# The last gate columns and the output projection go into the ordered list of a two-layer decoder trunk, with two of eight pairs of the projection by seven products

## Chip, cores and metric

The kernel runs on one core of one Trainium2 chip. The metric is the device time of one execution in microseconds; of several runs the median is taken. The engines are called as in the profile: PE is the matmul engine (TensorE), DVE is VectorE, ACT is ScalarE, POOL is GpSimd, and SP (SyncE) issues the DMAs.

## What is computed

The trunk has two layers over 256 tokens of width 2048. Each layer projects the normalised input to 6160 columns, runs eight gated linear-attention heads (GLA) and eight stick-breaking heads on them, joins their outputs, projects them back (`w_o`), and adds a squared-ReLU MLP:

```python
h = rms_norm(x, attn_norm)
g_q, g_k, g_v, g_gate, g_lr, s_q, s_k, s_v = split(h @ w_in)
...
o_gla = rms_norm(gla_chunked(...), gla_out_norm) * silu(g_gate)   # 1024 columns
o_sb  = rms_norm(stick_breaking_attention(...), sb_out_norm)      # 1024 columns
mixed = concatenate([o_gla, o_sb], axis=-1)
x = x + mixed @ w_o                                               # 2048 x 2048
hm = rms_norm(x, mlp_norm)
x = x + square(relu(hm @ w_up)) @ w_down                          # 8192 wide
```

The change touches the gate columns `g_gate`, the product `mixed @ w_o`, and how both stand to the MLP behind them.

## The kernel before

**Products.** A float32 product is made of three matmuls: weights are split into a high part (ACT, `whi`) and the rest (DVE, `wlo`), activations likewise, and a block is high x high, high x low and low x high. A matmul has 128 rows of the activation (one of two halves of the tokens, `tt`) against 512 weight columns.

**Attention part.** `unit` (L537) makes 512 columns of a projection: four loads of 512 rows of weights (1 MB each), each split in two parts, each part 12 matmuls; after each part a counter ticks, and small work that was put on the counter with `after` (head matmuls, transposes, norms) is issued there. A unit sums into one accumulator `acc`; there are two of them, of two PSUM banks each, taken in turn, beside four single banks `ps` (L197). Late in a layer come two units of GLA values (L1036), which bring `gla_pair` and `gla_out` of the last pairs; two units of gate columns (L1050); and four units of the output projection (L1077). `gate_part` (L1054) copies a unit's two banks out on ACT (L1056), makes the silu on ACT and DVE, and `gated` multiplies an `on` tile by it, which `to_operand` turns on PE into the operand `mixed`. Each of the first three projection units is added to the residual by one DVE instruction (L1075), then transposed for the MLP (`norm_operand`) and squared; the fourth is left to the list.

**Ordered list.** The MLP is written as pieces with an engine, a length and dependencies (class `Plan`, L40). `plan.run` walks a model of time, gives each ACT or DVE piece a due time from the PE pieces that need it, and writes out the instructions of PE, DVE and ACT in the order in which the model began them: whenever an engine comes free in the model, it takes the piece with the earliest due time among those that are ready at that moment. The pieces of PE and SP keep the order in which they were added. PE's last five parts ahead of the list stand in it as five pieces of 12 matmuls (`tail`, L1111), a load has 2.9 us on SP and lands 4.6 us later, an ACT piece of one part has 1.0, of one bank 0.55, and 0.06 us passes between engines.

The list's units have 1024 columns and eight pairs of 128-row blocks, four alternating passes of `w_up` and `w_down`. A plain pair (`steps`, L1200) has two parts of 12 matmuls, 24 in all, into banks 2, 4, 3 and 8. A fast pair (1, 3 and 5) has seven products in place of eight, 21 matmuls, into all eight banks m1 to m8: three sums of weight blocks on DVE (L1098, tiles `ts`, `raw`, `t`), four parts instead of two, sums of the operand's blocks (`forms`, L401), and at the end of a unit `down_tail` or `up_tail`, where the seven sums are combined.

**Memory.** Tiles with names in `ATT` (among them `kdz`, `v4` and `on`) and in `MLP` (among them `raw2`, `whi5`, `wlo5`) lie in one stretch of SBUF by turns; `open_scope` closes one set and opens the other. The list's first load of every four goes to `raw2`, its first part of every five to `whi5` and `wlo5`. `mlp_psum` (L204) closes the accumulators and opens the banks in the order m5, m7, m1, m6, m2, m4, m3, m8. These pools are opened with `reuse_waits="tile"`: a tile of the new pool waits for the old tiles whose memory it takes. Before, the SBUF set is opened ahead of the second projection unit, `mlp_psum` behind the fourth.

Of the kernel before, what the change touches and what calls it, by code (L numbers as in the profile page):

```python
# [17 lines left out]
P = 128  # L18
# [108 lines left out]
def trunk_kernel(  # L127
# [270 lines left out]
    def fast(i):  # L398
        return i in (1, 3, 5)
# [334 lines left out]
    def norm_pair(po):  # L734

        o = tmp("on", [P, 512], bufs=4)
# [39 lines left out]
    for l in range(DEPTH):  # L776
# [234 lines left out]
        def gla_out(e, v, vc, S, sc):  # L1011
# [21 lines left out]
            ons[e] = norm_pair(po)  # L1033
# [6 lines left out]
        def gated(e, gate, c):  # L1040
            o = ons[e]
            o4 = o.rearrange("p (h t d) -> p h t d", h=2, t=NT)
            for tt in range(NT):
                nc.vector.tensor_tensor(
                    o4[:, :, tt, :], o4[:, :, tt, :],
                    gate[:, tt, c : c + 2 * P].rearrange("p (h d) -> p h d", d=P), ALU.mult,
                )
            after(1, lambda: to_operand(mixed, e, o, gain("gla", l)))

        for g in range(2):  # L1050
            ug = unit(hT, wl, 0, C_GG + g * 512, 512)
            gate = act_tile(F32, (P, NT, 512))

            def gate_part(tt, ug, gate):  # L1054
                gx = gate[:, tt, :]
                nc.scalar.activation(gx, ug[:, tt, :], AF.Copy, scale=rst[:, tt : tt + 1])  # L1056
                e = tmp("t2", [P, 512], bufs=4)
                nc.scalar.activation(e, gx, AF.Abs)
                nc.scalar.activation(e, e, AF.Exp, scale=-1.0)
                nc.scalar.activation(e, e, AF.Ln, bias=1.0)  # L1060
                nc.vector.scalar_tensor_tensor(e, gx, 0.0, e, ALU.min, ALU.subtract)
                nc.scalar.activation(e, e, AF.Exp)
                nc.vector.tensor_tensor(gx, gx, e, ALU.mult)

            gate_part(0, ug, gate)
            after(1, lambda a=ug, b=gate: gate_part(1, a, b))
            for hp in range(2):
                after(3 + hp, lambda e=2 * g + hp, t=gate, c=hp * 2 * P: gated(e, t, c))


        hm = Operand()
        ssq = new_ssq()

        def residual(n, acc):
            nc.vector.tensor_tensor(xb[n], acc, xb[n], ALU.add)  # L1075

        for n in range(4):  # L1077
            uo = unit(mixed, w_o[l], 0, n * 512, 512, (2, 3, 0, 1))
            if n == 0:

                open_scope("sbuf", mlp=1)
            if n < 3:
                residual(n, uo)
                after(1, lambda n=n: norm_operand(hm, n, "mlp", l, sums=True))
                after(2, lambda n=n: norm_squares(n, ssq))
# [3 lines left out]
        mlp_psum()  # L1089
        hT = Operand()  # L1090
# [12 lines left out]
        units = [(q, down, n2) for q in range(4) for down in range(2) for n2 in range(2)]  # L1103
# [7 lines left out]
        tail = [add("PE", 12 * MM, None) for _ in range(RING)]  # L1111
        for t in tail:
            whi.append([t])
            wlo.append([t])
        x3 = add("DVE", V2, lambda: residual(3, uo), tail)

        def norm_last():

            sq = add("ACT", 2 * A1, lambda: norm_squares(3, ssq), x3)
            return norm_end(sq, ssq)  # L1120
# [13 lines left out]
        def turned(n, h2, m, op, key, ll, deps):  # L1134

            turn, high, low, _ = operand_parts(op, n, h2, key, ll, lambda: bank(m))
            a = add("PE", 8 * TR / 2, turn, deps, free.get(m))
# [5 lines left out]
        def weights(u, j):  # L1143
            q, down, n2 = units[u]
            if down:
                r0, c0, w = q * 2048, n2 * 1024, w_down[l]
            else:
                r0, c0, w = 0, q * 2048 + n2 * 1024, w_up[l]
            r0 += 2 * j * P
            return w[r0 : r0 + 2 * P, c0 : c0 + 1024].rearrange("(k p) n -> p k n", p=P)  # L1150

        def load(x):

            box = []

            def fn():
# [4 lines left out]
                nc.sync.dma_start(box[0], weights(*divmod(x, 8)))  # L1161
# [38 lines left out]
        def steps(x, r, ld, readers):  # L1200

            u, j = divmod(x, 8)
            q, down, n2 = units[u]
            op = up[q] if down else hm

            def blk(k, tt):
                sl = slice(tt * P, (tt + 1) * P)
                return lambda: (op.t[j][:, k, 0, sl], op.t[j][:, k, 1, sl])

# [3 lines left out]
            if not fast(j):  # L1213
# [57 lines left out]
        def down_tail(u):  # L1271
            q, _, n2 = units[u]
            end = q == 3 and l + 1 == DEPTH
# [44 lines left out]
        def up_tail(u):  # L1318
# [37 lines left out]
            def turn(h):  # L1356

                q, _, n2 = units[u]
# [5 lines left out]
                for i, m in enumerate(((5, 7), (1, 6))[h]):  # L1364
# [24 lines left out]
                    def made(k, box=box, h=h, i=i, pair=pair):  # L1389
                        key = "f", h, i  # L1390
                        if key not in box:
# [103 lines left out]
```

## Time and profile before

| | before |
|---|---|
| median of 3 runs | 2189.72 us (2189.27 to 2190.19) |
| profiled execution, its own time | 2190.13 us |
| span in its profile, first to last instruction | 2188.4 us |
| PE busy | 2180.2 us |
| DVE busy | 1795.7 us |
| ACT busy | 1255.3 us |
| mean granted PE clock | 1.000 |

The profiled execution takes 1.73 us more than the span that its profile shows, and is 0.41 us above the median. A row of a timeline gives the start in the span, the duration, engine, line, operation, tiles (out<-in), and in brackets the idle time ahead of it with what ended that. A matmul's duration is longer than the distance to the next one, since they overlap.

### The profile page before, as it was taken

Reading aid. Unit: us, or ns where it says so; the run is one execution under the profiler, and the core shown is the slowest. Engines: PE = TensorE matmul, PEld = TensorE weight load, DVE = VectorE, ACT = ScalarE, POOL = GpSimd, SP = SyncE. Lnnn points to the kernel's source line nnn. Section 1 sums busy time; section 2 is a strip of 40 time slices with the busy share of each in tenths; the row PEclk is TensorE's granted clock in tenths of the full one; section 3 lists DMA queues with packets and bytes.
Section 4 is the critical chain, followed back from the end, with each engine's and each line's share of the span. In section 5 each row is a group of like instructions: output and inputs, shape, how many; then the busy total and the mean of one; then the engine's idle time right before and its main releaser. Section 6 shows DMA issues by size and latency. Waiting matters only on the chain.

```text
span 2188.4 us, 27082 instructions
## 1 busy us (share of the span) xinstructions
PE 2180.2 (100%) x10376; PEld 1808.0 (83%) x10376; DVE 1795.7 (82%) x2286; ACT 1255.3 (57%) x1623; POOL 38.0 (2%) x64
## 2 busy tenths in 40 slices
PE   9999999999999999999999999999999999999999
PEld 7988778888888888888888887788888888888887
DVE  5777566799999999999957775567999999999998
ACT  5555346566566566466645553555665655665663
POOL 0020000000000000000000200000000000000000
PEclk9999999999999999999999999999999999999999
DMA  6654445566556556656546544465656665565564
GB/s 224 198 160 154 154 150 196 177 206 211 184 199 204 186 198 205 211 187 198 173 156 193 173 155 154 135 219 185 211 174 208 198 209 192 193 211 183 201 199 149
DMA packets 152549, 408.96 MB, mean 187 GB/s; under 512 B 6650, under 2 KB 31810, under 8 KB 152420
## 3 DMA queue, kind: packets, MB, share of 16 engines
q1 hardware_dynamic: 152420, 407.24, 56.7%
q8 instruction: 81, 1.33, 0.2%
q14 instruction: 48, 0.39, 0.1%
HBM read 405.12 MB, written 2.10 MB: 186 GB/s over the span
## 4 chain that ended last, share of the span: by engine, by line
PE 98%; DVE 1%; DMA 0%; issue 0%; ACT 0%; SPq 0%; POOL 0%; ACTq 0%
PE acc L549 9%; PE acc L551 9%; PE acc L550 9%; PE acc L596 3%; PE acc L600 1%; PE ps L1017 1%; PE ps L1029 1%; PE ps L441 0%; PE ps L976 0%; PE ps L712 0%; PE ps L658 0%; PE ps L747 0%; PE ps L676 0%; DMA raw<-in_w_in_dram 0%; PE ps L993 0%
## 5 line engine op out<-in xcount | busy, mean ns | idle before, releaser
L1180 ACT ACTIVATE whi<-raw 128x1024 fp32r<-128x1024 f32 x512 | 533.1, 1058 | 314.5 <-ACT whi L1180 12.1
L1184 DVE TENSOR_TENSOR wlo<-raw,whi 128x1024 fp32r<-128x1024 f32 x512 | 620.2, 1220 | 88.9 <-ACT whi L1180 84.8
L532 DVE TENSOR_TENSOR wlo<-raw,whi 128x1024 fp32r<-128x1024 f32 (+2 forms) x274 | 317.4, 1164 | 192.8 <-ACT whi L530 192.1
L530 ACT ACTIVATE whi<-raw 128x1024 fp32r<-128x1024 f32 (+2 forms) x274 | 273.6, 1005 | 292.6 <-PE acc L551 243.8
L549 PE MATMUL acc<-whi,act 128*128 128x512 f32 (+2 forms) x960 | 368.7, 384 | 1.3 <-ACT act L451 1.3
L550 PE MATMUL acc<-wlo,act 128*128 128x512 f32 (+2 forms) x960 | 362.3, 377 | 0.0
L551 PE MATMUL acc<-whi,act 128*128 128x512 f32 (+2 forms) x960 | 362.2, 377 | 0.0
L549 PEld LDWEIGHTS acc<-whi,act 128*128 128x128 f32 x960 | 181.2, 189 | 36.3 <-issue 4.1
L551 PEld LDWEIGHTS acc<-whi,act 128*128 128x128 f32 x960 | 180.8, 188 | 34.1 <-issue 0.7
L550 PEld LDWEIGHTS acc<-wlo,act 128*128 128x128 f32 x960 | 181.2, 189 | 31.1 <-issue 0.7
L1180 ACT ACTIVATE whi<-t 128x512 fp32r<-128x512 f32 x96 | 60.5, 630 | 151.6 <-DVE t L1098 150.0
L1184 DVE TENSOR_TENSOR wlo<-ts,whi 128x1024 fp32r<-128x1024 f32 x96 | 117.4, 1223 | 1.5 <-ACT whi L1180 0.3
L1098 DVE TENSOR_TENSOR ts<-raw 128x1024 f32<-128x1024 f32 x96 | 117.1, 1220 | 1.3
L1180 ACT ACTIVATE whi<-ts 128x1024 fp32r<-128x1024 f32 x96 | 101.0, 1052 | 27.4 <-PE m__662_3602 L1265 0.7
L596 PE MATMUL acc<-act,whi 128*128 128x512 f32 x256 | 91.9, 402 | 0.0
L600 PE MATMUL acc<-act,wlo 128*128 128x256 f32 x256 | 71.8, 280 | 0.0
L1184 DVE TENSOR_TENSOR wlo<-t,whi 128x512 fp32r<-128x512 f32 x96 | 65.7, 684 | 1.1 <-ACT whi L1180 1.1
L1098 DVE TENSOR_TENSOR raw<-ts,raw 128x512 f32<-128x512 f32 x96 | 65.6, 684 | 0.0
L1098 DVE TENSOR_TENSOR t<-raw 128x512 f32<-128x512 f32 x96 | 65.6, 684 | 0.0
L1349 ACT ACTIVATE act<-act,st 128x512 f32<-128x512 f32 x64 | 44.3, 716 | 26.5 <-DVE act L1098 26.5
L596 PEld LDWEIGHTS acc<-act,whi 128*128 128x128 f32 x256 | 48.1, 188 | 11.1
L600 PEld LDWEIGHTS acc<-act,wlo 128*128 128x128 f32 x256 | 48.4, 189 | 0.1
(2401 smaller groups left out, 4581.2 us busy)
## 6 DMA issues: line engine op xcount, KB each, us to landing
raw<-in_w_up_dram SPq DMA_DIRECT2D x128, 1024.0 KB, 5.1
raw<-in_w_down_dram SPq DMA_DIRECT2D x128, 1024.0 KB, 5.2
raw<-in_w_in_dram SPq DMA_DIRECT2D x84, 1024.0 KB, 5.2
raw<-in_w_o_dram SPq DMA_DIRECT2D x32, 1024.0 KB, 5.1
raw<-in_w_in_dram SPq DMA_DIRECT2D x14, 512.0 KB, 6.6
raw<-in_w_in_dram SPq DMA_DIRECT2D x8, 544.0 KB, 3.8
out_dram<-xb SPq DMA_DIRECT2D x8, 256.0 KB, 3.2
xb<-in_x_dram SPq DMA_DIRECT2D x3, 512.0 KB, 7.9
```

What stands on the lines that cost most here:

```text
L530: newest["hi"] = nc.scalar.activation(h, r, AF.Copy).ins
L532: newest["lo"] = nc.vector.tensor_tensor(lo[:, q : q + step, :width], r, f32(h), ALU.subtract).ins
L549: nc.tensor.matmul(o, xh[:, sl], whi[:, j, :width], start=first, stop=False)
L550: nc.tensor.matmul(o, xh[:, sl], wlo[:, j, :width], start=False, stop=False)
L551: st["mm"] = nc.tensor.matmul(o, xl[:, sl], whi[:, j, :width], start=False, stop=last).ins
L596: nc.tensor.matmul(acc[:, f, :], whi[:, j, sl], op.both(k), start=(k == 0), stop=False, skip_group_check=True,)
L600: nc.tensor.matmul(acc[:, f, T:], wlo[:, j, sl], xh, start=False, stop=(k == KT - 1), skip_group_check=True,)
L1017: nc.tensor.matmul(o, sc[:, (2 * tt + j) * P : (2 * tt + j + 1) * P], v[:, tt, vc + j * P : vc + (j + 1) * P], start=first, stop=False, sk ...
L1098: nc.vector.tensor_tensor(dst, a, b, op)
L1180: nc.scalar.activation(box["h"][:, :n], src(), AF.Copy)
L1184: nc.vector.tensor_tensor(box["l"][:, :n], src(), f32(box["h"][:, :n]), ALU.subtract)
L1349: nc.scalar.activation(box[h][:, tt, :], box[h][:, tt, :], AF.Relu, scale=rr[:, tt : tt + 1],)
```

## The change

The second unit of gate columns and the whole output projection become pieces of the ordered list, ahead of the MLP: one unit `g` of four loads (into m1 and m6), and two units `o` of 1024 columns, which run through the plain and fast steps, with `down_tail` adding them to the residual. In each `o` unit pairs 0 and 1 are fast, the other six plain, and the pairs of the stick-breaking heads (4 to 7) come first. The copies of the first gate unit (`copy_first`) and both silus are pieces as well. `mlp_psum` is called behind the second of these copies. The list's SBUF set opens right behind the first gate unit. `norm_pair` writes the GLA outputs to act tiles instead of `on`.

```diff
-            ons[e] = norm_pair(po)
+            if e % 2 == 0:
+                ons["t", e // 2] = act_tile(F32, (P, 2, 512))
+            ons[e] = norm_pair(po, ons["t", e // 2][:, e % 2, :])
...
-        for g in range(2):
-            ug = unit(hT, wl, 0, C_GG + g * 512, 512)
-            gate = act_tile(F32, (P, NT, 512))
...
+        ug = unit(hT, wl, 0, C_GG, 512)
+        gates_t = [act_tile(F32, (P, NT, 512))]
+        assert not held
+        open_scope("sbuf", mlp=1)
...
-        for n in range(4):
-            uo = unit(mixed, w_o[l], 0, n * 512, 512, (2, 3, 0, 1))
...
-        mlp_psum()
...
-        units = [(q, down, n2) for q in range(4) for down in range(2) for n2 in range(2)]
+        units = [("g", 0, 0), ("o", 0, 0), ("o", 0, 1)]
+        units += [(k, q, n2) for q in range(4) for k in ("up", "down") for n2 in range(2)]
+
+        def pair_order(u):
+
+            if units[u][0] != "o":
+                return range(8), {j for j in range(8) if fast(j)}
+            if units[u][2] == 0:
+                return (4, 5, 6, 7, 0, 1, 2, 3), {0, 1}
+            return (4, 5, 6, 0, 7, 1, 2, 3), {0, 1}
...
-        tail = [add("PE", 12 * MM, None) for _ in range(RING)]
...
-        x3 = add("DVE", V2, lambda: residual(3, uo), tail)
...
+        before = [add("PE", 12 * MM, None) for _ in range(RING)]
...
+        def copy_first(tt):
+            nc.scalar.activation(
+                gates_t[0][:, tt, :], ug[:, tt, :], AF.Copy, scale=rst[:, tt : tt + 1]
+            )
+            if tt:
+                mlp_psum()
+
+        for tt in range(NT):
+            gate_done[0, tt] = add(
+                "ACT", A1, lambda tt=tt: copy_first(tt), before[-3], gate_done.get((0, 0))
+            )
...
+            if kind == "g":
+                for s in range(2):
+                    yield parts(
+                        lambda s=s: r()[:, s, :].rearrange("p (c n) -> p c n", c=2),
+                        readers, ld,
+                    ), [(m, [(blk(k, tt, 2 * j + s), k) for k in range(2)])
+                        for tt, m in enumerate((1, 6))]
+                return
...
+                a = add("ACT", 3 * A1, logs, gate_done[g, tt], before[-1])
+                b = add("DVE", V1, least, a)
...
+                m = (5, 7)[hp]
...
+                a = add("DVE", 0.7, gated, ends)
+                turns.append((g, 4 * TR, turn, a, m, e, high, low, scaled, box))
+
+        def turn_gated():
+
+            g, cost, turn, a, m, e, high, low, scaled, box = turns.pop(0)
+            p = add("PE", cost, turn, a, free[m])
+            if e < 2:
+                b = add("ACT", A1, scaled, p)
+                free[m] = [b]
+                done["o", 0, e] = made(lambda: forms(mixed, e, box[1], "sx"), None, True, b)
...
+                    if kind == "g" and k == 4 or kind == "o" and n2 == 0 and k == 5:
+                        turn_gated()
+                        turn_gated()
...
+                    if k < 2 and was == ("o", 0, 0) or was == ("o", 0, 1) and k < 2:
+                        n = 2 * was[2] + k
                         for h2 in range(2):
-                            done["hm", 6 + h2] = turned(
-                                3, h2, (5, 7)[h2], hm, "mlp", l, x3
+                            done["up", 0, 2 * n + h2] = turned(
+                                n, h2, ((5, 7), (1, 6))[k][h2], hm, "mlp", l, sums=True
                             )
```

## Rows read from the trace of the kernel before

**Rows 1.** The page: busy time and instructions of each engine; the chain by engine.
```profile
PE 2180.2 (100%) x10376; PEld 1808.0 (83%) x10376; DVE 1795.7 (82%) x2286; ACT 1255.3 (57%) x1623; POOL 38.0 (2%) x64
...
PE 98%; DVE 1%; DMA 0%; issue 0%; ACT 0%; SPq 0%; POOL 0%; ACTq 0%
```

**Rows 2.** Waits of PE over the whole span: total, times, longest in us.
```profile
PE ps L499 <- POOL ident masks.py:199: 1.5, 1, 1.5
PE acc L549 <- ACT act L451: 1.3, 1, 1.3
...
PE m__1812_8943 L1264 <- DVE wlo L1184: 0.4, 1, 0.4
```

**Rows 3.** Busy time by stretches: gates and projection of each layer, then the MLP.
```profile
304.50:421.50 117.00, 117.00 (x541) 97.12 (x540) 74.79 (x94) 67.36 (x101) 0.00 (x0) 1.00 0.56 189
1392.00:1509.00 117.00, 117.00 (x542) 97.13 (x541) 74.92 (x94) 67.43 (x102) 0.00 (x0) 1.00 0.56 189
...
462.00:504.00 42.00, 42.00 (x195) 34.96 (x194) 39.98 (x52) 28.08 (x37) 0.00 (x0) 1.00 0.60 201
```

**Rows 4.** Timeline of PE where the first gate unit ends (start us, us).
```profile
304.04 0.39 PE L550 MATMUL acc<-wlo,act 128*128 128x512 f32 x1
304.27 0.39 PE L551 MATMUL acc<-whi,act 128*128 128x512 f32 x1
304.50 0.39 PE L549 MATMUL acc<-whi,act 128*128 128x512 f32 x1
```

**Rows 5.** Groups of DVE instructions by line and form: busy us, mean ns | idle before.
```profile
L1184 DVE TENSOR_TENSOR wlo<-raw,whi 128x1024 fp32r<-128x1024 f32 x512 | 620.2, 1220 | 88.9 <-ACT whi L1180 84.8
...
L1098 DVE TENSOR_TENSOR ts<-raw 128x1024 f32<-128x1024 f32 x96 | 117.1, 1220 | 1.3
L1184 DVE TENSOR_TENSOR wlo<-t,whi 128x512 fp32r<-128x512 f32 x96 | 65.7, 684 | 1.1 <-ACT whi L1180 1.1
L1098 DVE TENSOR_TENSOR raw<-ts,raw 128x512 f32<-128x512 f32 x96 | 65.6, 684 | 0.0
...
L1075 DVE TENSOR_TENSOR xb<-acc,xb 128x1024 f32<-128x1024 f32 x8 | 9.8, 1224 | 7.4 <-PE acc L551 7.4
```

**Rows 6.** Timeline of ACT from 301 us, and the same place in layer 2.
```profile
301.98 1.06 ACT L530 ACTIVATE whi<-raw 128x1024 fp32r<-128x1024 f32 x1 [0.21 <-PE acc L551]
304.70 1.27 ACT L1056 ACTIVATE act<-acc,st 128x512 f32<-128x512 f32 x2 [1.66 <-PE acc L551]
...
307.93 1.15 ACT L1060 ACTIVATE t<-t 128x512 f32<-128x512 f32 x2
308.98 1.06 ACT L530 ACTIVATE whi<-raw 128x1024 fp32r<-128x1024 f32 x1
...
1392.06 1.27 ACT L1056 ACTIVATE act<-acc,st 128x512 f32<-128x512 f32 x2 [1.66 <-PE acc L551]
```

**Rows 7.** Groups of ACT instructions: the gate copy and the split of one part.
```profile
L1180 ACT ACTIVATE whi<-raw 128x1024 fp32r<-128x1024 f32 x512 | 533.1, 1058 | 314.5 <-ACT whi L1180 12.1 <-PE acc L551 6.6 <-PE m__3210_15918 L1265 5.8
...
L1056 ACT ACTIVATE act<-acc,st 128x512 f32<-128x512 f32 x8 | 5.1, 686 | 6.6 <-PE acc L551 6.6
```

**Rows 8.** Timeline at 1077 us, all engines: PE begins again after a wait.
```profile
1077.38 1.22 DVE L1184 TENSOR_TENSOR wlo<-raw,whi 128x1024 fp32r<-128x1024 f32 x1
...
1077.88 0.39 PE L1263 MATMUL m__1812_8943<-whi,act 128*128 128x512 f32 x1
...
1078.65 0.50 PE L1264 MATMUL m__1812_8943<-wlo,act 128*128 128x512 f32 x1 [0.38 <-DVE wlo L1184]
...
1078.98 0.39 PE L1265 MATMUL m__1812_8943<-whi,act 128*128 128x512 f32 x1
```

**Rows 9.** Timeline of PE: last readers of `kdz` and of `S` and `v4`.
```profile
290.83 0.44 PE L976 MATMUL ps<-v,kdz 128*64 128x128 f32 x4
...
298.56 0.44 PE L1029 MATMUL ps<-S,act 128*64 128x128 f32 x4
```

**Rows 10.** The page's DMA issues: count, KB each, median us to landing.
```profile
raw<-in_w_in_dram SPq DMA_DIRECT2D x84, 1024.0 KB, 5.2
```

More of the change, by code (lines that the diff above doesn't have):

```diff
@@ L1271, in down_tail @@
         def down_tail(u):
-            q, _, n2 = units[u]
-            end = q == 3 and l + 1 == DEPTH
+            kind, q, n2 = units[u]
+            end = kind == "down" and q == 3 and l + 1 == DEPTH
             x11, x21, x12, x22 = (
@@ L1356, in turn @@
             def turn(h):
-                q, _, n2 = units[u]
+                _, q, n2 = units[u]
                 op = up.setdefault(q, Operand())
@@ L1387, in turn @@
                     pair = 4 * n2 + 2 * h + i
-                    def made(k, box=box, h=h, i=i, pair=pair):
-                        key = "f", h, i
-                        if key not in box:
-                            box[key] = forms(op, pair, box["t", h][:, i], "sx")
-                        box[key][k]()
-                    e = sq
-                    if fast(pair):
-                        e = add("DVE", 1.25, lambda f=made: f(0), sq)
-                    b = add("ACT", A1 * (2 if fast(pair) else 1), lambda f=made: f(1), e)
@@ new lines, in g_tail, with copy @@
+        def g_tail(p):
+            gates_t.append(None)
+            def copy(tt, m):
+                if tt == 0:
+                    gates_t[1] = act_tile(F32, (P, NT, 512))
+                nc.scalar.activation(
+                    gates_t[1][:, tt, :], banks[m], AF.Copy, scale=rst[:, tt : tt + 1]
+                )
+            for tt, m in enumerate((1, 6)):
+                free[m] = [gate_done.get((1, 0))]
+                gate_done[1, tt] = add("ACT", A1, lambda a=(tt, m): copy(*a), p[m], free[m])
+                free[m] = [gate_done[1, tt]]
+            gate(1)
@@ L1406, in trunk_kernel @@
         for m in (5, 7, 1, 6, 2, 4, 3, 8):
             free[m] = []
-        lastf = max(j for j in range(8) if fast(j))
+        hT_now, hT = hT, Operand()
         rr = rr_done = None
-        tails = {}
-        for u, (q, down, n2) in enumerate(units):
-            tails[u] = (down_tail if down else up_tail)(u)
-            begun, p, k = set(), {}, 0
-            for j in range(8):
-                x = 8 * u + j
-                r, ld, readers = load(x)
-                for (box, h, lo), prods in steps(x, r, ld, readers):
-                    ready = done.get((q, j) if down else ("hm", j))
-                    for m, blocks in prods:
-                        begin, end = m not in begun, j == (7 if m in (2, 4, 3, 8) else lastf)
+        turns, tails = [], {}
@@ new lines, in trunk_kernel @@
+        gate(0)
+        for u, (kind, q, n2) in enumerate(units):
+            order, quick = pair_order(u)
+            if kind != "g":
+                tails[u] = (up_tail if kind == "up" else down_tail)(u)
+            begun, p, k = set(), {}, 0
+            lasts = [j for j in order if j in quick][-1]
+            for j in range(4) if kind == "g" else order:
+                final = j == (3 if kind == "g" else order[-1])
+                r, ld, readers = load(u, j)
+                for (box, h, lo), prods in steps(u, j, j in quick, r, ld, readers):
+                    ready = done.get((kind, q, j))
+                    for m, blocks in prods:
+                        begin = m not in begun
+                        if kind == "g":
+                            end = final and k == 7
+                        else:
+                            end = final if m in (2, 4, 3, 8) else j == lasts
```

196 lines of the change are left out of this document (121 added, 75 removed).

## The prediction

> **What bounds the kernel now.** I read the page first: PE is busy for 2180.2 us of the 2188.4 us span, and the chain that ends last is 98% PE [rows 1]. Durations of matmuls overlap, so a full PE row alone doesn't prove that nothing waits. The list of PE's waits does: six entries, none over 1.5 us, of which one lies in an MLP (0.4 us) and none between the first gate unit and the MLP [rows 2]. The stretches say the same of the place that the change touches: from 304.5 to 421.5 us, 117 us, PE has no idle time, DVE works 74.8 us and ACT 67.4; the second layer repeats it to 0.2 us [rows 3]. So the time can only fall by what PE is given less, and rises by each wait that is new. What a matmul is worth is its distance to the next one, 0.227 us (304.04, 304.27, 304.50), not its duration of 0.39 [rows 4].
>
> **What PE loses.** The four projection units are 16 row blocks x 2 token halves x 3 matmuls x 4 = 384 matmuls a layer. The two new units have six plain pairs of 24 and two fast ones of 21, 186 each and 372 together. That is 12 fewer a layer, 24 in all: 24 x 0.2267 = 5.44 us. The second gate unit keeps its 96. The transposes are the same in number (16 of gated outputs, 32 for the MLP operand a layer) and only move. PE has no idle time to swallow the gain, so 5.44 us is what the change can bring at most.
>
> **What the other engines get, at no cost.** DVE, per fast pair and unit: three sums (1.22 + 0.68 + 0.68 us) and four splits (3 x 1.22 + 0.68) in place of two splits (2.44), 4.5 us more [rows 5], x 4 a layer = 18.0. The tails: 12 additions of 0.68 in each of two units, 16.4, less four residuals of 1.22 [rows 5], +11.5. The sums of two operand pairs, 896 columns each: 2.4 us at 0.68 per 512 columns, up to 4.1 as six steps of 0.68, of which I take 3.3, since they are short steps. Together +32.8 us a layer, so 74.8 + 32.8 = 107.6 us in a stretch that becomes 117 - 2.7 = 114.3 us: 94%. In the MLP 42 us of PE work hold 40.0 us of DVE work, 95%, without a wait of PE [rows 3]. The stretch is as dense as that and no denser, and I cost it at nothing; what covers it is that parts are made up to five ahead of PE. If the cover fails, the price is the wait that the first MLP has at 1077.9 us: 1078.65 where the beat would have it at 1078.11, and one more late step behind, 0.65 us [rows 8]. I keep 0 to 0.65 us a layer. ACT gets less than DVE and has 50 us free. The silu chain of the first gates has four ACT and two DVE steps per half behind the copies, then the products with the GLA outputs: eight steps of 0.52 us (two take 1.15 in a row [rows 6]) and eight of at most 0.68 [rows 5], 10 us if nothing overlapped. It is asked for 13.6 us (five parts of 12 matmuls) into the `g` unit; that of the second has six parts, 16.3 us. Both are hidden; if one were not, PE would wait for the difference.
>
> **DMAs and memory.** The list's first load goes to `raw2`, which now lies over `kdz` and the older `v4` (it is the first tile asked for from the new set). It therefore waits until the last `gla_pair` has read `kdz`, at 291.3 us [rows 9], lands 5.2 us later [rows 10], 296.5, and three loads stand behind it on SP. `whi5` lies over both `v4`, read by PE until 299.0 [rows 9]. ACT is free for the first part at 301.8, where before it splits a part at 301.98 [rows 6], and needs 1.06 us. So the load has 5 us to spare and is free; later than that, each us is paid by PE. On POOL nothing new is queued; in layer 2 its clearing of `kdz` waits for `raw2` instead of an earlier tile, some 200 us ahead of use.
>
> **The new wait.** This is the term that decides. The first gate unit is the 14th accumulator of its layer (seven units, four of `unit_t`, two of values ahead of it), so it has the second buffer, the third and fourth bank. `mlp_psum` opens m5, m7, m1, m6 first, so m1 and m6 are that third and fourth bank, and m1 and m6 are where the `g` unit begins. Before, the next unit took the other buffer and went on at 304.50 without a break [rows 4], while ACT copied the banks out, from 304.70 [rows 6]. Now PE must wait for these copies. The two copies take 1.27 us in a row [rows 6], 0.69 each [rows 7], so one begins 0.585 us after the other. They cannot start earlier: the row at 304.70 was idle for 1.66 us until the unit's last matmul [rows 6].
>
> Nor are they adjacent any more. In the list's model the copies are ready after three of the five pieces ahead, 3 x 2.724 + 0.06 = 8.23 us. The first load is there at 2.9 + 4.6 + 0.06 = 7.56, so ACT splits the first part from 7.56 to 8.56. At 8.56 it takes what is ready: the first copy is, while the second part becomes ready in the same instant, one event later. Then the second part is ready and the second copy not. The order on ACT is: part 1, copy 1, part 2, copy 2, part 3. On the chip copy 1 stands waiting for PE, and behind it part 2 and copy 2; PE waits for copy 2, as the accumulator is one tile and a tile of the new pool waits for all of the old one.
>
> Price: copy 1 at 304.70; part 2 at 305.28, for 1.06 us [rows 7]; copy 2 about 0.10 us before that ends, since an instruction starts that much before its predecessor ends (308.98 against 307.93 + 1.15) [rows 6], so 306.24 to 306.93. PE starts 0.05 us after the end that it waits for (1078.65 against 1077.38 + 1.22), and the matmul after that comes 0.11 us late (1078.98 - 1078.65 against 0.227) [rows 8]. 306.98 - 304.50 + 0.11 = 2.59 us a layer, 5.18 us in all; the second layer has the same rows at 1392.06 [rows 6]. The parts behind it are in time: part 3 is split by 307.9 and asked for at 312.4.
>
> A page of the Trainium skill speaks against this place: Perfetto Trace Analysis, section Optimizing Tensor Performance, Matmuls, says that independent groups of matmuls should rotate through different PSUM banks, so that the emptying of one overlaps the next. Rows 4 and 6 agree for the kernel before, where the copies run beside the next unit; with the `g` unit in the free buffer the sum would be the whole -5.44 us.
>
> **Sum.** -5.44 + 5.18 = -0.26 us. Against the profiled execution of 2190.13 us that is 2189.87; the median lies 0.41 us below that execution, so the forecast is 2189.5 us. With the DVE waits it goes up to 2190.8.
>
> **Rivals.**
> 1. *Bank by bank.* PE waits for copy 1 alone at m1: 304.70 + 0.69 + 0.05 = 305.44, 0.94 us late plus 0.11. Six matmuls later, 306.91, it wants m6, free at 306.98: 0.18 more. 1.23 us a layer, 2.46 in all: -2.98, 2186.7 us. For it: the copies read one bank each. Against: the rule of the pool in the code is by tile, and copy 1 itself waited for the whole unit before, not for its own bank [rows 6]. Beside it stands the Trainium skill's page PSUM — Partial Sum Buffer, section PSUM bank collisions raise a hardware error: accesses need to be guarded by bank, which these two copies would meet one by one.
> 2. *Copies in a row.* If part 2 comes before or behind both, PE goes on at 304.70 + 1.27 + 0.05 = 306.02: 1.63 us a layer, -2.18, 2187.5 us.
> 3. *No wait.* If the banks don't meet, all 5.44 us remain: 2184.3 us. Against it stand the count of accumulators and the order of the banks.
> 4. *DVE sets the pace* (slower). In the new units the splits and sums of a fast pair come too late for PE, as at 1077.9 us, but at every fast pair: 8 x 0.65 = 5.2 us [rows 8] on top of the bank wait: +4.9, 2194.7 us. For it: the first `w_up` unit now carries the second projection's last additions and the operands of four pairs beside its three fast pairs. Its parts (5 x 2.44 + 3 x 6.93 = 33.0) and some 10.5 us of additions (eight of 0.68) and operand work are 43.5 us of durations against 41.5 us of matmuls and 16 transposes. Against it: durations overlap a little, and stretches with nearly that load ran without a wait [rows 3]. It decides from the point where DVE falls five parts behind.
>
> **How the numbers follow.** Forecast 0.51, bank by bank 0.15, in a row 0.12, no wait 0.09, DVE 0.13. A measurement of this kernel tells about 0.2%, 4.4 us, from no change: faster is below 2185.3, slower above 2194.1. Faster holds the case without a wait and a tail of the first rival, 0.11; slower most of the DVE case, 0.11; the rest, 0.78, is the same. The range must reach the cases at 2184.3 to keep four fifths, and at the top the forecast with DVE waits in both layers and once more, 2192.0; it leaves out the DVE case alone.
>
> **What would show it.** PE has 24 fewer matmuls, 10352. Two new entries in its waits, of about 2.3 us idle each (306.98 against the end of the last matmul at 304.66), the first matmul of m1 released by the act tile of a copy on ACT, with the order part, copy, part, copy in ACT's timeline. DVE about 33 us busier per layer in the stretch, 94%, with no PE wait on `wlo` above 0.7 us. I am wrong if that wait is near 0.9 or 1.5 us (rivals 1 and 2), if it is absent, if PE waits for `wlo` or `ts` at fast pairs of the projection, or if the first load lands after 301.8 us and copy 1 stands behind it.

## The result and the profile after

| | before | after |
|---|---|---|
| median | 2189.84 us (2188.15 to 2190.67, 21 runs) | 2193.34 us (2190.89 to 2194.06, 21 runs) |
| ratio, 95% interval | 1 | 1.0014 (1.0007 to 1.002) |
| profiled execution, its own time | 2190.13 us | 2193.46 us |
| span in its profile | 2188.4 us | 2191.8 us |

The kernel became 3.5 us slower, where -0.3 us was forecast; 2193.34 is 1.3 us above the top of the range. The change of 0.14% by the ratio lies inside the 0.2% that was called the same, but its interval excludes zero. One thing is needed to understand the number: 6 of the 21 executions had a mean granted PE clock of 1.000 and took 2190.89 to 2191.24 us, the other 15 had 0.999 or 0.998 and took 2192.51 to 2194.06, with a median of 2193.4.

The page of after, engines and chain [rows 1]:

```profile
PE 2178.1 (99%) x10352; PEld 1804.7 (82%) x10352; DVE 1851.6 (84%) x2386; ACT 1275.4 (58%) x1651; POOL 37.9 (2%) x64
...
PE 98%; DVE 1%; issue 0%; ACT 0%; DMA 0%; SPq 0%; POOL 0%; ACTq 0%
```

PE has its 24 matmuls less, and DVE works 1851.6 us where it worked 1795.7. The bound is still PE. What PE waits for in after (total, times, longest in us) [rows 2]:

```profile
PE m__2417_11934 L1282 <- ACT act L1089: 2.4, 1, 2.4
PE m__530_2766 L1282 <- ACT act L1089: 2.4, 1, 2.4
...
PE m__2602_12866 L1283 <- DVE wlo L1195: 0.4, 1, 0.4
...
PE m__1855_9038 L1283 <- DVE wlo L1195: 0.4, 1, 0.4
PE m__715_3698 L1283 <- DVE wlo L1195: 0.4, 1, 0.4
```

Four entries are new: two of 2.4 us, one in each layer, for the copy of the first gate unit (now L1089), and two of 0.4 us for `wlo` (now L1195; the three matmuls are L1282 to L1284). The wait for m__1855 is the one that before has at 1078.65 [rows 8]. The place of the first wait in after's timeline, PE and ACT (start us, us):

```profile
304.24 0.39 PE L551 MATMUL acc<-whi,act 128*128 128x512 f32 x1
304.72 0.69 ACT L1089 ACTIVATE act<-acc,st 128x512 f32<-128x512 f32 x1 [2.04 <-PE acc L551]
305.31 1.05 ACT L1191 ACTIVATE whi<-raw 128x1024 fp32r<-128x1024 f32 x1
306.25 0.68 ACT L1089 ACTIVATE act<-acc,st 128x512 f32<-128x512 f32 x1
...
306.98 0.50 PE L1282 MATMUL m__530_2766<-whi,act 128*128 128x512 f32 x1 [2.36 <-ACT act L1089]
...
307.32 0.39 PE L1283 MATMUL m__530_2766<-wlo,act 128*128 128x512 f32 x1
```

Copy, part, copy: the order that was worked out, and PE begins at 306.98, to the hundredth as forecast. The row at 304.24 is the last matmul of the first gate unit, which before has at 304.27 [rows 4]. Here is the same place in layer 2, PE alone; the fence behind it is a table of stretches (start:end, length, then busy us and instructions of PE, PEld, DVE, ACT, POOL, the granted clock, DMA share, GB/s).

```profile
1392.63 0.39 PE L551 MATMUL acc<-whi,act 128*128 128x512 f32 x1
1395.38 0.80 PE L1282 MATMUL m__2417_11934<-whi,act 128*128 128x512 f32 x1 [2.36 <-ACT act L1089]
1395.97 0.63 PE L1283 MATMUL m__2417_11934<-wlo,act 128*128 128x512 f32 x1
1396.40 0.63 PE L1284 MATMUL m__2417_11934<-whi,act 128*128 128x512 f32 x1
```

```profile
307.00:310.00 3.00, 3.00 (x13) 2.51 (x14) 2.70 (x3) 2.97 (x4) 0.00 (x0) 1.00 0.42 85
307.00:424.00 117.00, 117.00 (x541) 97.43 (x541) 104.44 (x145) 78.30 (x114) 0.00 (x0) 1.00 0.56 189
...
424.00:442.00 18.00, 17.64 (x77) 13.54 (x76) 17.89 (x25) 11.07 (x16) 0.00 (x0) 1.00 0.50 169
...
1396.00:1397.00 1.00, 1.00 (x4) 0.81 (x3) 0.70 (x2) 1.00 (x2) 0.00 (x0) 0.50 0.00 0
...
1399.00:1402.00 3.00, 3.00 (x15) 2.46 (x14) 2.02 (x3) 2.94 (x6) 0.00 (x0) 1.00 1.02 389
```

Both waits have the same 2.36 us. What follows differs: behind the first PE goes on at once at full clock, 0.227 us from matmul to matmul; behind the second the granted clock is 0.50, 1.2 GHz instead of 2.4, and the matmuls stand 0.43 us apart (1395.97, 1396.40) until 1398.5; the stretch from 1399 us is at 1.00 again. The Trainium skill, page TensorE: Matmul & The Clock Gate, section Part 1: The HAM clock gate (the "warmup" mystery), gives 426.7 ns from start to start for 512 columns at the lower clock; the rows agree.

The projection's stretch (307 to 424 us) has 104.4 us of DVE work, 89% of it, against 74.8 us in [rows 3]: 29.6 us more, where 32.8 more and 94% had been worked out. PE has no wait in it. The new waits for DVE lie behind it, in the first `w_up` unit, where DVE is busy for 17.89 of 18.00 us. The rows of PE and DVE there:

```profile
428.26 0.47 PE L1282 MATMUL m__747_3831<-whi,sxh 128*128 128x512 f32 x1
428.57 0.39 PE L1283 MATMUL m__747_3831<-wlo,sxh 128*128 128x512 f32 x1
...
439.51 0.39 PE L1282 MATMUL m__715_3698<-whi,act 128*128 128x512 f32 x1
440.25 0.51 PE L1283 MATMUL m__715_3698<-wlo,act 128*128 128x512 f32 x1 [0.36 <-DVE wlo L1195]
```

```profile
437.85 1.22 DVE L1058 TENSOR_TENSOR ts<-raw 128x1024 f32<-128x1024 f32 x1
438.98 1.22 DVE L1195 TENSOR_TENSOR wlo<-raw,whi 128x1024 fp32r<-128x1024 f32 x1
```

At 439.51 a plain part's split (438.98, ends 440.20) stands on DVE behind the sum of a fast pair (437.85): PE loses 0.52 + 0.11 us. Ahead of that, between 427 and 437, six matmuls come 0.03 to 0.11 us late, 0.39 us together; the step from 428.26 to 428.57 is one of them.

**Where the 3.3 us between the two profiles are.** From that last gate matmul to the span's end, before takes 2188.41 - 304.27 = 1884.14 us and after 2191.76 - 304.24 = 1887.52: +3.38, so all of it lies behind that point. In layer 1 after has: 12 matmuls less -2.72, bank wait 2.52 + 0.11 = +2.63, DVE 0.63 + 0.39 = +1.02, together +0.93; it took 796.34 us to the next layer's first matmul where before took 795.37. Layer 2 takes 1091.18 against 1088.77, +2.41: the same +0.96 and 1.45 more, which are the matmuls at half clock (the step behind the wait is 0.36 us over the usual 0.227 where 0.11 is usual behind a wait, six more are 0.20 over it: 0.25 + 1.20).

### The profile page after: what moved, and what is told of

It reads as the page before. It is cut to its first block, busy times and chain, and to the rows that moved or that the text cites. A ratio compares the mean times of both kernels' runs of the same rounds, so it can differ in the third digit from the quotient of the medians.

```text
span 2191.8 us, 27186 instructions
## 1 busy us (share of the span) xinstructions
PE 2178.1 (99%) x10352; PEld 1804.7 (82%) x10352; DVE 1851.6 (84%) x2386; ACT 1275.4 (58%) x1651; POOL 37.9 (2%) x64
## 4 chain that ended last, share of the span: by engine, by line
PE 98%; DVE 1%; issue 0%; ACT 0%; DMA 0%; SPq 0%; POOL 0%; ACTq 0%
PE acc L549 6%; PE acc L551 6%; PE acc L550 6%; PE acc L596 3%; PE acc L600 1%; PE ps L1017 1%; PE ps L1029 1%; PE ps L976 0%; PE ps L712 0%; PE ps L658 0%; PE ps L676 0%; DVE wlo L1195 0%; DMA raw<-in_w_in_dram 0%; PE m__2417_11934 L1282 0%; PE ps L441 0%
## 5 line engine op out<-in xcount | busy, mean ns | idle before, releaser
L1191 ACT ACTIVATE whi<-raw 128x1024 fp32r<-128x1024 f32 x592 | 616.5, 1057 | 351.0 <-ACT whi L1191 11.6
L1195 DVE TENSOR_TENSOR wlo<-raw,whi 128x1024 fp32r<-128x1024 f32 x592 | 718.1, 1221 | 98.1 <-ACT whi L1191 93.2
L532 DVE TENSOR_TENSOR wlo<-raw,whi 128x1024 fp32r<-128x1024 f32 (+2 forms) x194 | 220.5, 1140 | 133.5 <-ACT whi L530 133.3
L530 ACT ACTIVATE whi<-raw 128x1024 fp32r<-128x1024 f32 (+2 forms) x194 | 189.8, 983 | 206.2 <-PE acc L551 155.9
L549 PE MATMUL acc<-whi,act 128*128 128x512 f32 (+2 forms) x640 | 243.0, 380 | 1.2 <-ACT act L451 1.2
L550 PE MATMUL acc<-wlo,act 128*128 128x512 f32 (+2 forms) x640 | 237.9, 372 | 0.0
L551 PE MATMUL acc<-whi,act 128*128 128x512 f32 (+2 forms) x640 | 237.5, 371 | 0.0
L549 PEld LDWEIGHTS acc<-whi,act 128*128 128x128 f32 x640 | 121.2, 189 | 24.1 <-issue 4.1
L551 PEld LDWEIGHTS acc<-whi,act 128*128 128x128 f32 x640 | 120.9, 189 | 21.3 <-issue 0.7
L550 PEld LDWEIGHTS acc<-wlo,act 128*128 128x128 f32 x640 | 121.1, 189 | 18.9 <-issue 0.7
L1195 DVE TENSOR_TENSOR wlo<-ts,whi 128x1024 fp32r<-128x1024 f32 x104 | 127.3, 1224 | 7.3 <-ACT whi L1191 6.4
L1058 DVE TENSOR_TENSOR ts<-raw 128x1024 f32<-128x1024 f32 x104 | 127.1, 1222 | 1.3
L1195 DVE TENSOR_TENSOR wlo<-t,whi 128x512 fp32r<-128x512 f32 x104 | 71.6, 688 | 2.8 <-ACT whi L1191 2.8
```

Of the source, the lines that this page charges most:

```text
L530: newest["hi"] = nc.scalar.activation(h, r, AF.Copy).ins
L532: newest["lo"] = nc.vector.tensor_tensor(lo[:, q : q + step, :width], r, f32(h), ALU.subtract).ins
L549: nc.tensor.matmul(o, xh[:, sl], whi[:, j, :width], start=first, stop=False)
L550: nc.tensor.matmul(o, xh[:, sl], wlo[:, j, :width], start=False, stop=False)
L551: st["mm"] = nc.tensor.matmul(o, xl[:, sl], whi[:, j, :width], start=False, stop=last).ins
L1058: nc.vector.tensor_tensor(dst, a, b, op)
```

## Experiments

The beginning of the span differs between executions of any of these kernels: the last matmul of the first gate unit stands at 301.95 us in one profile and 304.82 in another, with the same matmuls ahead of it, and a median carries that too. The profiles are therefore also compared by the **rest**: the time from that matmul to the span's end. Times of before are those of the same chip: 2189.41 us for the first four kernels, 2188.84 for the next four, 2189.10 for the last four.

| kernel | time us (lowest to highest, runs) | ratio to before, 95% | rest us | against before's 1884.14 |
|---|---|---|---|---|
| after | 2193.34 (2190.89 to 2194.06, 21) | 1.0014 (1.0007 to 1.002) | 1887.52 | +3.38 |
| e1_other_banks | 2187.16 (2186.58 to 2188.32, 11) | 0.9991 (0.9982 to 1.0) | 1882.21 | -1.93 |
| e2_copies_in_a_row | 2188.52 (2187.97 to 2190.15, 11) | 0.9998 (0.9989 to 1.0007) | 1884.06 | -0.08 |
| e3_pe_kept_busy | 2191.50 (2190.62 to 2192.22, 11) | 1.0008 (1.0 to 1.0017) | 1886.06 | +1.92 |
| e4_longer_wait | 2198.12 (2197.32 to 2199.91, 5) | 1.004 (1.0028 to 1.0053) | 1892.37 | +8.23 |
| e5_plain_pair_first | 2185.78 (2184.65 to 2186.82, 11) | 0.9986 (0.9977 to 0.9994) | 1880.84 | -3.30 |
| e6_three_fast | 2200.55 (2199.88 to 2201.76, 5) | 1.0052 (1.0038 to 1.0065) | 1895.20 | +11.06 |
| e7_one_fast | 2186.85 (2185.94 to 2187.85, 11) | 0.9989 (0.998 to 0.9998) | 1881.88 | -2.26 |
| e8_wait_in_before | 2192.48 (2191.32 to 2194.11, 11) | 1.0016 (1.0007 to 1.0024) | 1887.52 | +3.38 |
| e9_after_again | 2192.97 (2189.68 to 2193.98, 11) | 1.0015 (1.0007 to 1.0024) | 1886.02 | +1.88 |
| e10_wait_layer1 | 2188.80 (2188.03 to 2192.13, 11) | 1.0001 (0.9992 to 1.001) | 1884.12 | -0.02 |
| e11_wait_layer2 | 2189.09 (2188.47 to 2190.87, 11) | 1.0002 (0.9993 to 1.0011) | 1885.74 | +1.60 |
| e12_kept_busy_again | 2191.44 (2189.98 to 2192.58, 11) | 1.001 (1.0001 to 1.0018) | 1886.09 | +1.95 |

**Theory A:** the bank wait has the price that was worked out, and behind a wait of that length the clock can fall, which makes the rest of the loss. **Rivals:** B, the lower clock has another cause than the wait; C, another late input stands behind the banks; D, DVE sets the pace, and waits that are moved from one place come back at another; E, the wait belongs to the change of pools and not to the bank; F, the two groups of times come from the chip of the first runs; G, only the wait of the second layer lowers the clock.

**e1: no shared banks.** The `g` unit goes to m5 and m7, which lie in the free accumulator, and the gated transposes to m1 and m6.

```diff
-                        for tt, m in enumerate((1, 6))]
+                        for tt, m in enumerate((5, 7))]
...
-                m = (5, 7)[hp]
+                m = (1, 6)[hp]
...
-            for tt, m in enumerate((1, 6)):
+            for tt, m in enumerate((5, 7)):
```

> The g unit sums into m5 and m7 and the gated outputs are turned in m1 and m6; nothing else. Theory A (PE's wait for the two copies costs 2.6 us a layer, and the lower granted clock behind it in layer 2 comes from that wait): both waits of 2.4 us go, 5.2 us, and with them the stretch at clock 0.50; against the changed kernel's 2193.3 us that is 2193.3 - 5.2 - 2.3 = 2185.8 us, clock 1.000 in every run. Rival B (the lower clock comes from something else at the head of the list): only the 5.2 us go, 2188.1 us, and two thirds of the runs stay at 0.999. Rival C (the list's head has another late input behind the banks): PE waits for a split part instead, more than 2189 us.

2187.16 us, between what A and B expect, with the clock at 1.000 in all eleven executions: B, which kept the lower clock, falls here. Both 2.4 us waits are gone. The longest of PE's waits that are left behind the start (total, times, longest), and two rows of the timeline of layer 1, of PE and of its weight loads (PEld):

```profile
PE m__1855_9038 L1283 <- DVE wlo L1195: 0.4, 1, 0.4
...
PE m__2602_12866 L1283 <- DVE wlo L1195: 0.4, 1, 0.4
```

```profile
306.15 0.50 PE L1283 MATMUL m__528_2764<-wlo,act 128*128 128x512 f32 x1
...
317.16 0.31 PEld L1461 LDWEIGHTS m__530_2766<-ident,act 128*128 128x128 f32 x3 [0.20 <-DVE act L1449]
```

The prediction weighed the Trainium skill's rule that independent groups rotate through banks (Perfetto Trace Analysis, Optimizing Tensor Performance, Matmuls); this run agrees, at 1.9 us a layer (rest 1882.21 against 1886.02 for the changed kernel at full clock, e9). The wait itself is 2.63; 0.7 us of it come back in and behind the `g` unit, which now runs earlier against ACT and DVE. A low part is late (305.67 to 306.15, 306.49: 0.36 us over the usual steps), and the transposes of the gated outputs wait for DVE's products (316.94, 317.55, 318.14: steps of 0.61 and 0.59 us, where e9 has 0.43 and 0.36). In this small size C holds. And free banks alone don't bring -5.44 us: of the 2.72 us that a layer saves, 1.75 go to delays that before doesn't have.

**e2: the copies in a row.** Both are one ACT piece, in the old banks.

```diff
-        for tt in range(NT):
-            gate_done[0, tt] = add(
-                "ACT", A1, lambda tt=tt: copy_first(tt), before[-3], gate_done.get((0, 0))
-            )
+        gate_done[0, 0] = gate_done[0, 1] = add(
+            "ACT", 2 * A1, lambda: (copy_first(0), copy_first(1)), before[-3]
+        )
```

> Both copies of the first gate unit are one piece, so no part is split between them; the banks stay. Both theories of the wait expect PE idle 1.4 us instead of 2.4 at the head of the list, 1.63 us a layer instead of 2.59: 1.9 us less. Theory A (the clock falls because of the wait): the shorter wait leaves the clock at 1.000, 2191.0 - 1.9 = 2189.1 us. Rival B (the clock falls for another reason): two thirds of the runs still at 0.999, 2191.4 us.

2188.52 us, clock 1.000 in all eleven. PE's waits of this kernel:

```profile
PE m__527_2760 L1281 <- ACT act L1089: 1.4, 1, 1.4
PE m__2414_11928 L1281 <- ACT act L1089: 1.4, 1, 1.4
```

```profile
304.20 0.50 PE L1281 MATMUL m__527_2760<-whi,act 128*128 128x512 f32 x1 [1.42 <-ACT act L1089]
```

The wait is shorter by 0.94 us a layer (2.36 to 1.42); the rest is 1.96 us less than that of e9, 0.98 a layer, where 0.96 was worked out. So PE waits for the second copy wherever it stands, and the part between the copies costs what the prediction's second rival said.

**e3 and e12: PE kept at work in the wait.** Twenty transposes into a bank that nothing reads are added, useless work that fills most of the wait and leaves its end where it is.

```diff
             if tt:
                 mlp_psum()
+                pw = bank(5)
+                for _ in range(20):
+                    nc.tensor.transpose(pw[:, :P], ident, ident)
```

> The wait stays as it is, but PE turns the identity 20 times into the free bank m5 while it lasts (about 2.2 us of otherwise useless transposes). Theory A (the clock falls because PE stands idle): clock 1.000 in every run, and the time of the changed kernel's runs at clock 1.000, 2191.0 us, plus at most 0.2. Rival B: the share of runs at 0.999 does not change, median 2193.3 us.

> The kernel with 20 transposes of a spare bank that keep PE at work during most of the wait, once more, beside the changed kernel on the same chip. Theory A: clock 1.000 in all executions, +1.5 to 2 us against before, below the changed kernel's median by 1 to 2.4 us. Rival (the clock isn't what parts the two groups): the same two groups as the changed kernel.

2191.50 and 2191.44 us, clock 1.000 in all 22 executions. Both medians lie a little above what A allowed: e3 by 0.3 us, e12, at +2.3 us against before, by the same. The wait in e12, PE's timeline:

```profile
302.63 0.39 PE L551 MATMUL acc<-whi,act 128*128 128x512 f32 x1
302.86 2.34 PE L1096 MATMUL m__528_2764<-ident 128*128 128x128 f32 x20
305.38 0.50 PE L1285 MATMUL m__530_2766<-whi,act 128*128 128x512 f32 x1 [0.18 <-ACT act L1089]
```

From 302.63 to 305.38 are 2.75 us, as from 304.24 to 306.98 in after (2.74): the wait is as long, only PE isn't idle in it. On the same chip e12 lies 1.5 us below the unfilled kernel (e9, 2192.97), and its rest, 1886.09, is that of e9's profiled execution, which was one without a fall, to 0.07 us. So the clock follows PE's idle time and not the waiting as such.

**e4: a longer wait.** Two ACT copies into a scratch tile ahead of the second gate copy, also useless.

```diff
         def copy_first(tt):
+            if tt:
+                for _ in range(2):
+                    junk = tmp("t2", [P, 512], bufs=4)
+                    nc.scalar.activation(junk, xb[0][:, 0, :], AF.Copy)
```

> ACT copies two banks' worth of the residual into a scratch tile between the two copies (about 1.1 us of useless work), so PE stands idle 3.4 us instead of 2.4. Both expect 1.1 us more a layer, 2.2. Theory A (the clock falls because of the wait): the clock falls in every run, in both layers in most of them (mean clock 0.998), 2193.3 + 2.2 + up to 2.3 = 2195.5 to 2197.8 us. Rival B: the same share of runs at 0.999 as before, 2195.5 us.

2198.12 us, 0.3 us above A's range, mean clock 0.997 or 0.998 in all five. PE's waits, and stretches behind them in both layers:

```profile
PE m__532_2770 L1286 <- ACT act L1093: 3.4, 1, 3.4
PE m__2421_11942 L1286 <- ACT act L1093: 3.4, 1, 3.4
```

```profile
308.50:310.50 2.00, 2.00 (x7) 1.51 (x6) 1.84 (x2) 1.94 (x4) 0.00 (x0) 0.50 0.92 346
...
1398.50:1400.50 2.00, 2.00 (x6) 1.60 (x5) 1.66 (x2) 1.97 (x4) 0.00 (x0) 0.50 0.88 238
1400.50:1402.50 2.00, 2.00 (x6) 1.52 (x6) 1.40 (x2) 1.97 (x4) 0.00 (x0) 0.50 0.90 303
```

1.04 us more idle time in each layer gives 2.1 us; the rest grew by 6.4 us against e9 (1892.37 against 1886.02), the other 4.3 being half clock in both layers, longer in the second.

**e9: the changed kernel once more.**

> The changed kernel once more, beside the three others of this batch on one chip. Theory A (the granted clock falls in a part of the executions behind PE's idle 2.36 us, and costs some 2.4 us of the time where it does): two groups of times again, about 1.5 us above before at mean clock 1.000 and about 3.9 us above before at 0.999, median between them or in the upper one. Theory F (the two groups came from the chip that the first runs were on): one group here.

Two groups again: three executions at mean clock 1.000 (2189.68 to 2190.69) and eight below (2192.10 to 2193.98, median 2193.4). The unfilled kernel does the same on another chip, so F falls. The profiled execution was one at 1.000, with the same wait and no fall behind it:

```profile
1390.35 0.39 PE L551 MATMUL acc<-whi,act 128*128 128x512 f32 x1
1393.10 0.50 PE L1282 MATMUL m__2417_11934<-whi,act 128*128 128x512 f32 x1 [2.36 <-ACT act L1089]
1393.44 0.40 PE L1283 MATMUL m__2417_11934<-wlo,act 128*128 128x512 f32 x1
```

Its rest is +1.88 us against before: that is the change at full clock.

**e10 and e11: the wait in one layer only.**

```diff
-                        for tt, m in enumerate((1, 6))]
+                        for tt, m in enumerate((5, 7) if l == 1 else (1, 6))]
...
-                m = (5, 7)[hp]
+                m = ((1, 6) if l == 1 else (5, 7))[hp]
...
-            for tt, m in enumerate((1, 6)):
+            for tt, m in enumerate((5, 7) if l == 1 else (1, 6)):
```

e11 has `l == 0` in these places.

> The second gate unit keeps its old banks (m1, m6, with the wait) in the first layer only; in the second it takes m5, m7, without a wait. Against before: e1, with no wait in either layer, was 2.3 us faster than before, one wait is 2.4 to 2.6. Theory A (each wait can drop the clock by itself, equally in both layers): about +0.2 us against before where the clock stays at 1.000, +2.6 where it falls, in some of the executions. Theory G (only the wait of the second layer drops it, as in the profiled execution of after): one group, +0.2 us, clock 1.000 in all.

> The mirror of the last: the wait only in the second layer. Theory A: as in the first layer, +0.2 or +2.6 us against before, in some of the executions. Theory G: all the drops are here, in about two of three executions, median about +2.6 us at 0.999.

In e10 three of eleven executions were below 1.000, in e11 two of eleven. G falls: the wait of either layer can do it. Those with a fall had medians 1.4 us (e10) and 1.7 us (e11) above the others. e11's profiled execution was one of them, and its layer 2 takes 1091.28 us against e9's 1089.73, +1.55. Two matmuls behind its wait, which ended at 1392.69 us, and its stretches:

```profile
1394.19 0.59 PE L1282 MATMUL m__2418_11935<-whi,act 128*128 128x512 f32 x1
1394.57 0.63 PE L1283 MATMUL m__2418_11935<-wlo,act 128*128 128x512 f32 x1
```

```profile
1395.00:1397.00 2.00, 2.00 (x6) 1.61 (x5) 1.51 (x2) 1.94 (x4) 0.00 (x0) 0.50 0.89 330
1399.00:1402.00 3.00, 3.00 (x15) 2.50 (x14) 2.61 (x4) 3.00 (x5) 0.00 (x0) 1.00 0.50 198
```

Here PE worked at the full rate for 1.5 us behind the wait, seven matmuls up to 1394.19, before the next stood 0.38 and then 0.43 us apart (to 1395.00): the fall can come when PE is already at work again, where in after it was there at the wait's end. Its price is also less than the 2.4 us that the expectations took from after's two groups.

What A did not say is the count: two waits that each do it in 3 or 2 of 11 executions would do it in 13 of 32; the changed kernel did in 23 of 32 (15 of 21 and 8 of 11). That stays open. One fall in an execution seems to be the rule: after's profile, with the lower clock in one layer, reads a mean of 0.999, e4's, with it in both, 0.998, and of those 23 executions 19 read 0.999 and four 0.998.

**e8: the wait in the kernel before.** A third accumulator, filled by one transpose and read by a small DVE copy, both useless, turns the second gate unit of before to the banks of the first; the second copy is issued at once.

```diff
         for g in range(2):
+            if g:
+                other = acc_tile()
+                nc.tensor.transpose(other[:, 0, :P], ident, ident)
             ug = unit(hT, wl, 0, C_GG + g * 512, 512)
+            if g:
+                nc.vector.tensor_copy(tmp("t2", [P, P], bufs=4), other[:, 0, :P])
...
-            after(1, lambda a=ug, b=gate: gate_part(1, a, b))
+            gate_part(1, ug, gate)
```

> The kernel before, with an idle accumulator (one useless transpose into it, one small copy out of it a layer) so that the second gate unit has to take the banks of the first, and both copies of the first issued at once. Theory A (the bank is what PE waits for at the head of the list, and the list has no part in it): a new PE wait of 1.4 us for the act tile in each layer, 1.63 us of time plus 0.1 for the transpose, clock 1.000: before + 3.5 = 2192.9 us. Rival E (the wait belongs to the change of pools, not to the bank): no wait, before + 0.2.

2192.48 us, clock 1.000 in all eleven, rest +3.38, where 1.63 us a layer, with the copies in a row, was worked out. The wait comes without a change of pools, so E falls. PE's wait for both second gate units (L1061 is the copy in this kernel):

```profile
PE acc L549 <- ACT act L1061: 2.5, 2, 1.2
```

**e5, e7 and e6: what DVE costs, on top of e1.** e5 puts a second plain pair ahead of the first fast one in the first `w_up` and the last `w_down` unit of a layer; e7 and e6, both on top of e5, give the projection units one and three fast pairs instead of two.

```diff
             if units[u][0] != "o":
-                return range(8), {j for j in range(8) if fast(j)}
+                late = units[u] in (("up", 0, 0), ("down", 3, 1))
+                seq = (0, 2, 1, 3, 4, 5, 6, 7) if late else range(8)
+                return seq, {j for j in range(8) if fast(j)}
```

```diff
-                return (4, 5, 6, 7, 0, 1, 2, 3), {0, 1}
-            return (4, 5, 6, 0, 7, 1, 2, 3), {0, 1}
+                return (4, 5, 6, 7, 0, 1, 2, 3), {0, 1, 2}
+            return (4, 5, 6, 0, 7, 1, 2, 3), {0, 1, 2}
...
-            if e < 2:
+            if e < 3:
```

e7 has `{0}` and `e < 1` there.

> On top of e1_other_banks: in the first w_up unit and the last w_down unit pair 2 (plain) is taken ahead of pair 1 (fast). Theory A: the three waits for a low part that are left in e1 (0.65 us each, at 436, 1075 and 1522 us, all at the first plain pair behind the first fast one in a unit that also turns operands) come from DVE having that fast pair's work right behind the operands'; they go, 1.95 us: 2187.2 - 1.95 = 2185.2 us. Rival D (DVE has too much work in the unit as a whole): the waits only move to a later pair, 2187.2 us.

> On top of e5_plain_pair_first: only pair 0 of each projection unit by seven products, so 12 matmuls more over both layers and 18 us less of DVE work. Theory A (the matmuls left out are worth their distance, 0.227 us each): 2185.2 + 2.7 = 2187.9 us. Rival D (DVE work costs as much as the matmuls save): no change, 2185.2 us.

> On top of e5_plain_pair_first: pairs 0, 1 and 2 of each projection unit by seven products. 12 matmuls fewer a layer again, 24 x 0.227 = 5.44 / 2 = 2.72 us each layer, 5.44 in all per further... counted plainly: one more fast pair is 3 matmuls in each of 2 units and 2 layers, 12 matmuls, 2.72 us. Theory A (PE is the bound and DVE still hides): 2185.2 - 2.7 = 2182.5 us. Rival D (DVE is the bound once it has 4.5 us more in each projection unit, 18 us in all): PE waits for sums and low parts in the projection, the gain is eaten or more, 2184 to 2188 us.

e5: 2185.78 us, 3.1 us below before on its chip, and 1.4 us less rest than e1. The wait of the last `w_down` unit is gone (A). That of the first `w_up` unit is not: it stands at the fifth pair, behind the second fast one, in e1 (436.15 us) as in e5 (435.85), so the expectation had its place wrong. It grew from 0.36 to 0.52 us idle, while the six smaller delays ahead of it are gone; the unit loses 0.8 us a layer where it lost 1.0 (D, for the most part). PE's waits in e5:

```profile
PE m__716_3700 L1285 <- DVE wlo L1197: 0.5, 1, 0.5
PE m__2603_12868 L1285 <- DVE wlo L1197: 0.5, 1, 0.5
```

e7, between its two expectations, with 12 matmuls more than e5 (2.72 us), has no entry of an `m` bank that waits for DVE, and a rest 1.04 us longer: of what the second fast pair saves, 1.7 us go to DVE delays. e6, 12 matmuls less than e5, is 14.8 us slower, far from both expectations. A stretch of e6, and the longest of PE's waits in it:

```profile
410.00:452.00 42.00, 38.24 (x170) 29.98 (x170) 41.61 (x60) 26.55 (x43) 0.00 (x0) 1.00 0.52 175
```

```profile
PE m__645_3342 L1284 <- DVE xb L1058: 1.6, 1, 1.6
...
PE m__726_3716 L1285 <- DVE wlo L1197: 0.6, 1, 0.6
```

DVE has 41.61 of 42.00 us and PE 38.24: here DVE is the bound, and PE waits for the additions of `down_tail` as well. The prediction's fourth rival decides between two and three fast pairs; at the change itself it is the 1.0 us a layer of the first `w_up` unit. e6 also has four waits of 1.6 us, and the clock stayed at 1.000 in all five executions.

## Why the prediction was wrong

- **Right: what PE loses.** 24 matmuls fewer, 10352.
- **Right: the bank wait.** Order of ACT, place (306.98) and release as worked out; it cost 2.63 us a layer instead of 2.59. Rival 1, bank by bank, falls by after and e2: PE waited for the second copy each time. Rival 2 is what e2 and e8 did, and cost 1.66 us a layer in e8 (797.03 against 795.37 in layer 1) where 1.63 was worked out. Rival 3 is e1's edit, and didn't reach its 2184.3. The DMA term was right too: ACT splits the first part at 301.64 in after, as it comes free.
- **Failed: the price of the wait ends with "the matmul after that comes 0.11 us late".** That row comes from a wait of 0.38 us [rows 8] and was taken for one of 2.36; what the clock does behind the longer one was put at nothing, without a reason. The row holds in the executions whose clock stayed; in 23 of 32 (after and e9) the clock fell behind a wait, which cost 1.45 us in the profile of after. No wait (e1), one of 1.4 us (e2) and one filled with work (e3, e12) didn't lower the mean clock below 1.000 in any of 44 executions. No wait of before was longer than 1.5 us [rows 2], so its trace could not show the fall; a bound on it was left out of the range.
- **Mis-sized: DVE's term.** "I cost it at nothing", with 0 to 0.65 us a layer kept. It measured 1.02 in layer 1 and about as much in layer 2. The stretch that was costed was covered, as said; what was not is the unit behind it, which the prediction counted (43.5 us of durations against 41.5) for the fourth rival alone. Those 41.5 us are the 183 matmuls without the 16 transposes, which take 1.6 us more (two groups of 0.79 us from 417.24 and 420.86 in e9), so the unit was as good as full on both engines. The single wait there was the size taken from [rows 8]; six smaller delays came with it.
- **Sum.** At full clock -5.44 + 5.26 + about 2.0 = +1.8, measured +1.88 (e9's rest). With 1.45 us of half clock in one layer +3.3, measured +3.38 (after's rest). From before's median of 2189.84 the first alone gives 2191.7, inside the range; the second 2193.2, outside. The executions bear it out: the six of after at 1.000 took 2190.89 to 2191.24 us, inside the range, and the median fell among those with a fall.

What stays open: why one execution loses the clock behind a wait and another, with the same 2.36 us, doesn't; why two waits do it more often than one wait's count makes likely; and what makes up the 2.4 us between after's two groups, of which one fall, as profiled, is 1.45.

## To carry to other kernels

A new wait of a matmul engine that is otherwise never idle is priced in two terms: its length, and what the clock may lose behind it; if the profile shows no idle time of that length, keep the second in the range. Where a group of matmuls moves to other accumulators, see first which bank it starts in and who still reads it: two bank numbers were worth 1.9 us a layer here. And when work is given to an engine that is nearly full, look also at the stretch behind the one that it is given in: here the one costed had no wait, and the unit behind it lost 1.0 us a layer.

## What had not been expected of the hardware

The granted clock fell to 1.2 GHz behind 2.36 us without matmuls in some executions and not in others of the same program, behind 1.4 us (e2) in none of eleven and behind 1.6 us (e6) in none of five, and in both layers of the profile behind 3.4 us (e4). The first matmuls of the program differ in the same way from run to run: in before's profile they stand 0.43 us apart at 10.30, in e9's 0.23 at 9.40. Here the spacing alone shows it, since the profile's clock reads 1.00 for 10 to 12 us in both.

```profile
10.30 0.63 PE L549 MATMUL acc<-whi,act 128*128 128x512 f32 x1
10.72 0.63 PE L550 MATMUL acc<-wlo,act 128*128 128x512 f32 x1
```

```profile
9.40 0.40 PE L550 MATMUL acc<-wlo,act 128*128 128x512 f32 x1
9.63 0.40 PE L551 MATMUL acc<-whi,act 128*128 128x512 f32 x1
```

That is a part of the 2.3 us by which the last gate matmul differs between them (304.27 and 301.95), which is more than the whole change at full clock (1.88).
